# Sums of weight quadrants by accumulating transfers from GpSimd instead of VectorE additions, in one decoder layer on one Trainium2 core

## The chip, the cores and the metric

The kernel runs on one core of one Trainium2 chip. The metric is the device time of one execution in microseconds, the median of three runs. A core has five engines with instruction queues of their own, each in order: TensorE (PE in the profile, with its weight loads as PEld), VectorE (DVE), ScalarE (ACT), GpSimd (POOL) and SyncE (SP, whose queue issues transfers as SPq). They share an on-chip memory, and transfers to and from the large memory are carried by sixteen DMA engines. An engine's instruction waits on semaphores that other engines and transfers raise.

## The reference

One decoder layer on 512 tokens of width 2048, in float32. Cut to what matters here:

```python
mod = silu(c) @ w_ada + b_ada                      # shift, scale, gate
h = rms_norm(x, norm_w) * (1 + scale) + shift
proj = h @ w_in                                    # 2048 -> 21056 channels
a_out = swa_attention(...) * silu(ag)              # 32 query heads, window 128
y_a = a_out @ w_o_swa
o = gated_delta_rule(dq, dk, dv, g, beta)          # 16 key heads, 32 value heads, chunks of 64
y_b = (rms_norm(o, dn_norm_w) * silu(dz)) @ w_o_dn # 4096 -> 2048
y = sigmoid(mg_a) * y_a + sigmoid(mg_b) * y_b
out = x + gate * (y @ w_out)                       # 2048 -> 2048
```

## The kernel before

The 512 tokens lie on the free axis and the channels on the partitions. A channel tile (`channel_tile`) is 128 channels of `h @ w_in`: 16 blocks of the contraction, and for each three matmuls of 128x512 (`mm3`, L255 to L257), since a float32 product is made of a high and a low part (high x high, high x low, low x high). The weights come as 1 MB tiles `raw` (L213, two buffers), and ScalarE and VectorE split each half into `whi` and `wlo` (L61, L62; three buffers) ahead of use. TensorE's order is written out by the program; the rest of the work hangs beside it: `channel_tile` calls `pump` after every sixth matmul, eight times a tile, and `pump` steps generators. `go` starts one that asks for a delay in calls at each yield. `paced` starts one with a budget: each call adds the budget to a purse, and a step is taken when the purse holds what the last yield asked for. A recording layer then orders the instructions of each engine's queue and puts in the semaphores.

The stages in order: start-up (`h`, first tiles), keys of the delta rule with a triangular solve, attention, delta heads, the product with `w_o_dn`, the products with `w_o_swa` and `w_out`. The change is in the delta heads (`delta_heads`): 16 groups `g`, each with five channel tiles (one of queries, two of values, two of gates) and, beside them, its work: loads of the decay rows `E`, masks of them on GpSimd (L742), exponentials on ScalarE (L748), products with `pqk` on VectorE (L886), loads of `qe` and products `qe` on GpSimd (L880), small loads `tt`, `ta`, `lab`, `ts`, loads `k` and `kT`, and a scan over four chunks (`pp`, `pv`, `pod`); `ptq` is the transpose of the group's queries, once a group. `o_d` is where a group's result is stored.

The products with `w_o_dn` (in two halves) and `w_out` are made of seven smaller products each (`PRODUCTS`), on 2x2 blocks of the matrices, where four of the seven need a sum of weight blocks: with quadrants 00, 10, 11, 01 the sums are f0 = 00 + 10, f1 = 10 + 11, f2 = 00 + 10 + 11, f3 = all four. `weight_sums` makes them during the delta heads, from group 3 on, and stores them in `g_d` and `f_d`, from where the later stages load them as they load weights. A unit of it is one half of the columns (1024) of one block: four quadrant tiles `q` of 128x1024 are loaded by SP (L1193), VectorE adds (L1198, in place), and SP stores each sum (L1200). There are 24 units, with a budget of 2.0 a call. `behind` ties an instruction's place in its queue to the last matmul recorded, without a semaphore.

Of the kernel before, what the change touches and what calls it, by code (L numbers as in the profile page):

```python
# [7 lines left out]
F32 = mybir.dt.float32  # L8
# [3 lines left out]
ALU = mybir.AluOpType  # L12
# [4 lines left out]
P = 128  # L17
# [28 lines left out]
class Layer:  # L46
# [603 lines left out]
    def delta_heads(self):  # L650
        tc, nc = self.tc, self.nc
        with ExitStack() as sb:
            self.pmm = sb.enter_context(tc.tile_pool(name="pmmh", bufs=2, space=PSUM, reuse_waits="tile"))
            self.ptp = sb.enter_context(tc.tile_pool(name="ptph", bufs=3, space=PSUM, reuse_waits="tile"))
            self.psc = sb.enter_context(tc.tile_pool(name="psch", bufs=3, space=PSUM, reuse_waits="tile"))
            self.gwk = sb.enter_context(tc.tile_pool(name="gwkh", bufs=1, reuse_waits="tile"))
            wk = sb.enter_context(tc.tile_pool(name="dnB", bufs=2, reuse_waits="tile"))
            self.tt = []
            for n in range(4):
                t = wk.tile([P, NTB, P], F32, tag=f"tt{n}", name=f"tt{n}", bufs=1)  # L660
                nc.gpsimd.memset(t[HD:P, :, 0:HD], 0.0)
                self.tt.append(t)
            while not self.solved:
                self.step_slow(self.solves)
            ws = sb.enter_context(tc.tile_pool(name="wsum", bufs=1, reuse_waits="tile"))
            sums = None
            for g in range(KH):
                if g == 3:
                    sums = self.paced(self.weight_sums(ws), 2.0)
                if g == 8:  # L670
                    self.drain_slow(self.solves)
                self.heads(wk, g)
            for j in range(9, 12):
                self.merge_gate("ma", j, self.ma_d)
            self.drain_live()
            self.drain_slow(sums)

    def solve_all(self):
        for b in range(2):
# [498 lines left out]
            self.split(self.hh[:, kt, :], self.hl[:, kt, :], raw)  # L1178
            yield 1.2

    def weight_sums(self, wk):

        nc, a = self.nc, self.a
        sets = [(a["w_od"][0], self.g_d[0]), (a["w_od"][1], self.g_d[1]), (a["w_out"], self.f_d)]
        for w, dst in sets:
            for n in range(2):
                for i in range(2):
                    for h in range(2):
                        cols = slice(h * 1024, (h + 1) * 1024)
                        q = []  # L1190
                        for c, r in ((0, 0), (1, 0), (1, 1), (0, 1)):
                            t = wk.tile([P, 1024], F32, tag=f"q{c}{r}", name=f"q{c}{r}", bufs=1)
                            self.behind(nc.sync.dma_start(out=t, in_=w[2 * c + n, 2 * r + i][:, cols]))  # L1193
                            q.append(t)
                            yield 1.0
                        yield 8.0
                        for f, (x, y) in enumerate(((0, 1), (1, 2), (0, 2), (2, 3))):
                            self.behind(nc.vector.tensor_tensor(out=q[f], in0=q[x], in1=q[y], op=ALU.add))  # L1198
                            yield 6.0
                            self.behind(nc.sync.dma_start(out=dst[n, f, i][:, cols], in_=q[f]))  # L1200
                        yield 7.0

    def rope_tables(self, wk, keep):
        nc, a = self.nc, self.a
# [507 lines left out]
```

## Time and profile before

| what | value |
|---|---|
| runs | 2870.41, 2878.47, 2881.50 us; median 2878.47 |
| the profiled execution | 2872.04 us, its span 2870.2 us |
| TensorE busy, share of the span | 2820.4 us, 98% |
| VectorE busy | 1969.6 us, 69% |
| ScalarE busy | 1188.4 us, 41% |
| GpSimd busy | 141.6 us, 5% |
| DMA | 604.28 MB, mean 211 GB/s |
| additions of the sums (L1198) | 96, 124.5 us, from 1265.6 to 2118.5 us |
| loads and stores of the sums (L1193, L1200) | 96 and 96, 0.5 MB each |

The span runs from the first to the last instruction of the profiled execution; the execution's own time lies 1.8 us above it. The matmuls' ends are modelled, so that a busy TensorE is not one at its pace; the pace shows in the distance from one matmul to the next. The DMA share is the mean busy share of the sixteen DMA engines.

### The profile page before, as it was taken

How to read it: one execution, taken by the hardware profiler on the slowest of the kernel's cores; microseconds unless marked ns; L12 is line 12 of the kernel's file. 1: busy time of each engine (PE TensorE's matmuls, PEld its weight loads, DVE VectorE, ACT ScalarE, POOL GpSimd, SP SyncE). 2: the span in 40 equal slices, each digit the busy share in tenths (PEclk: the TensorE clock that was granted, in tenths of full speed). 3: DMA queues.
4: the chain of work that ended last, by engine and by line, in shares of the span. 5: the costliest groups of instructions: out<-in, count | busy, mean ns of one | idle time of the engine just before them, and what ended most of it. 6: DMA issues, size and time to landing. Idle time of an engine off the chain costs nothing.

```text
span 2870.2 us, 38671 instructions
## 1 busy us (share of the span) xinstructions
PE 2820.4 (98%) x14396; PEld 2314.6 (81%) x14396; DVE 1969.6 (69%) x3174; ACT 1188.4 (41%) x2382; POOL 141.6 (5%) x124
## 2 busy tenths in 40 slices
PE   7899999999999999999999999999999999999999
PEld 6588888877877778888788888888888888878887
DVE  7776776868768766778676666665656776664576
ACT  4356443234444343433433333333334454433443
POOL 0001000100001000001000000000000000000000
PEclk9999999999999999999999999999999999999999
DMA  9777864322252343456777676666646887885784
GB/s 398 289 250 235 257 231 143 112 89 90 80 159 81 110 151 99 134 170 233 236 261 246 229 241 232 235 236 228 231 171 226 288 314 258 295 281 175 245 317 165
DMA packets 227727, 604.28 MB, mean 211 GB/s; under 512 B 76081, under 2 KB 102193, under 8 KB 187089
## 3 DMA queue, kind: packets, MB, share of 16 engines
q1 hardware_dynamic: 227538, 601.81, 62.0%
q8 instruction: 113, 1.85, 0.3%
q14 instruction: 76, 0.62, 0.1%
HBM read 481.32 MB, written 118.17 MB: 209 GB/s over the span
## 4 chain that ended last, share of the span: by engine, by line
PE 87%; DVE 5%; DMA 3%; ACT 2%; issue 1%; SPq 0%; POOL 0%; DVEq 0%; POOLq 0%; ACTq 0%
PE mm L255 20%; PE mm L257 20%; PE mm L256 20%; PE m L256 5%; PE m L255 5%; PE m L257 5%; DVE wa L437 1%; DVE wlo L62 1%; PE pv L933 1%; DMA E<-g_rows 1%; PE S L1389 1%; PE pod L952 1%; PE O L1440 1%; PE pP L296 1%; ACT sm L1413 1%
## 5 line engine op out<-in xcount | busy, mean ns | idle before, releaser
L255 PE MATMUL mm<-hh,whi 128*128 128x512 f32 x2784 | 1130.1, 406 | 2.8 <-ACT mth L285 2.8
L257 PE MATMUL mm<-hh,wlo 128*128 128x512 f32 x2784 | 1089.5, 391 | 0.0
L256 PE MATMUL mm<-hl,whi 128*128 128x512 f32 x2784 | 1086.9, 390 | 0.0
L62 DVE TENSOR_TENSOR wlo<-raw,whi 128x1024 fp32r<-128x1024 f32 (+1 forms) x532 | 655.2, 1232 | 425.0 <-ACT whi L61 409.6
L61 ACT CAST whi<-raw 128x1024 fp32r<-128x1024 f32 (+1 forms) x532 | 555.4, 1045 | 848.6 <-PE mm L256 612.2
L255 PEld LDWEIGHTS mm<-hh,whi 128*128 128x128 f32 x2784 | 523.5, 188 | 113.6 <-issue 9.2
L257 PEld LDWEIGHTS mm<-hh,wlo 128*128 128x128 f32 x2784 | 522.6, 188 | 113.6 <-issue 0.5
L256 PEld LDWEIGHTS mm<-hl,whi 128*128 128x128 f32 x2784 | 524.0, 188 | 100.4 <-issue 1.4
L1198 DVE TENSOR_TENSOR q<-q,q 128x1024 f32<-128x1024 f32 x96 | 124.5, 1297 | 0.2 <-DMA q<-in_w_od 0.2
L748 ACT ACTIVATE E<-E,neg_g 128x128 f32<-128x128 f32 x256 | 82.1, 393 | 88.7 <-POOL E L742 88.6
L777 DVE TENSOR_TENSOR atmp<-A 128x62 f32<-128x62 f32 (+30 forms) x124 | 109.7, 884 | 0.5
L785 DVE TENSOR_TENSOR A<-A,atmp 128x62 f32<-128x62 f32 (+30 forms) x124 | 109.1, 880 | 0.4
L880 POOL TENSOR_TENSOR qe<-qe,yq 128x512 f32<-128x512 f32 x32 | 50.9, 1608 | 940.2 <-DMA qe<-eg_rows 624.3
L953 ACT COPY osb<-pod 128x256 f32<-128x256 f32 x64 | 23.8, 372 | 149.9 <-PE pod L952 149.9
L742 POOL TENSOR_SCALAR_AFFINE_SELECT E<-E 128x512 f32<-128x512 f32 x64 | 60.0, 950 | 430.7 <-DMA E<-g_rows 307.2
L935 ACT COPY vn<-pv 128x256 f32<-128x256 f32 x64 | 23.8, 372 | 120.8 <-PE pv L933 120.8
L1413 ACT ACTIVATE sm<-sm,mx,rs 128x256 f32<-128x256 f32 (+1 forms) x128 | 71.7, 562 | 3.5 <-DVE mx L1408 3.5
L604 DVE SCALAR_TENSOR_TENSOR yv<-mm,convh,yv 128x511 f32<-128x511 f32 (+2 forms) x96 | 71.4, 743 | 1.2
L940 DVE TENSOR_SCALAR vs<-vn,kd 128x128 f32<-128x128 f32 x96 | 23.1, 283 | 60.6 <-ACT vn L935 60.6
L437 DVE SCALAR_TENSOR_TENSOR wa<-wa,silu_cb 128x2048 f32<-128x2048 f32 x24 | 54.8, 2283 | 0.0
L963 DVE SCALAR_TENSOR_TENSOR S<-S,egl,pod 128x128 f32<-128x128 f32 x64 | 19.3, 343 | 50.8 <-ACT junk L956 50.8
L609 ACT ACTIVATE th<-yv 128x512 f32<-128x512 f32 x32 | 20.1, 628 | 72.7 <-DVE yv L604 72.7
(427 smaller groups left out, 3684.4 us busy)
## 6 DMA issues: line engine op xcount, KB each, us to landing
raw<-in_w_ch SPq DMA_DIRECT2D x158, 1024.0 KB
wa<-in_w_ada_ss SPq DMA_DIRECT2D x32, 1024.0 KB
q<-in_w_od SPq DMA_DIRECT2D x64, 512.0 KB
g_d<-q SPq DMA_DIRECT2D x64, 512.0 KB
raw<-g_d SPq DMA_DIRECT2D x32, 1024.0 KB
raw<-in_w_od SPq DMA_DIRECT2D x24, 1024.0 KB
gw<-in_w_ada_gate SPq DMA_DIRECT2D x16, 1024.0 KB
E<-g_rows SPq DMA_DIRECT2D x64, 256.0 KB
```

Source lines behind the costliest of these rows:

```text
L61: self.nc.scalar.copy(out=hi, in_=src)
L62: self.nc.vector.tensor_tensor(out=lo, in0=src, in1=hi.bitcast(F32), op=ALU.subtract)
L255: nc.tensor.matmul(ps, lhsT=wh, rhs=xh, start=first, stop=False)
L256: nc.tensor.matmul(ps, lhsT=wh, rhs=xl, start=False, stop=False)
L257: self.last_mm = nc.tensor.matmul(ps, lhsT=wl, rhs=xh, start=False, stop=last)
L437: nc.vector.scalar_tensor_tensor(out=wa, in0=wa, scalar=0.5, in1=scb, op0=ALU.mult, op1=ALU.mult, accum_out=t[:, j : j + 1])
L604: nc.vector.scalar_tensor_tensor(out=y[:, s:], in0=ps[:, : T - s], scalar=w[:, j : j + 1], in1=y[:, s:], op0=ALU.mult, op1=ALU.add)
L748: self.nc.scalar.activation(E[:, c, :], E[:, c, :], AF.Exp, bias=self.neg_g[:, c, h : h + 1])
L777: eng.tensor_tensor(out=t, in0=A[:, m : m + 1, m + 1 :].to_broadcast([P, m, n]), in1=A[:, :m, m : m + 1].to_broadcast([P, m, n]), op=ALU.mult,
L785: self.behind(eng.tensor_tensor(out=A[:, :m, m + 1 :], in0=A[:, :m, m + 1 :], in1=t, op=ALU.add))
L1198: self.behind(nc.vector.tensor_tensor(out=q[f], in0=q[x], in1=q[y], op=ALU.add))
L1413: nc.scalar.activation(t, t, AF.Exp, scale=r[:, h : h + 1], bias=mx[:, h : h + 1], accum_out=den[:, h : h + 1])
```

## The change

`weight_sums` is split in two generators, one for each half of the columns, and each walks the twelve blocks by itself, with a budget of 1.5. In each, two tiles are used for each block: tile 0 is loaded with quadrant 00, and quadrants 10, 11 and 01 are added to it one after another by transfers that accumulate into the tile as they land (`accum_op`), issued from GpSimd's queue; after each, the tile is stored (f0, f2, f3). Tile 1 is loaded with 10 and accumulates 11 (f1). VectorE has no part in it. A block's half has now two plain loads, four accumulating transfers and four stores, where a unit had four loads, four additions on VectorE and four stores. The tiles take the same space.

```diff
@@ delta_heads
-            sums = None
+            sums = []
             for g in range(KH):
                 if g == 3:
-                    sums = self.paced(self.weight_sums(ws), 2.0)
+                    sums = [self.paced(self.weight_sums(ws, p), 1.5) for p in range(2)]
...
-            self.drain_slow(sums)
+            for e in sums:
+                self.drain_slow(e)
@@ weight_sums
-    def weight_sums(self, wk):
+    def weight_sums(self, wk, part):
...
-                    for h in range(2):
-                        cols = slice(h * 1024, (h + 1) * 1024)
-                        q = []
-                        for c, r in ((0, 0), (1, 0), (1, 1), (0, 1)):
-                            t = wk.tile([P, 1024], F32, tag=f"q{c}{r}", name=f"q{c}{r}", bufs=1)
-                            self.behind(nc.sync.dma_start(out=t, in_=w[2 * c + n, 2 * r + i][:, cols]))
-                            q.append(t)
-                            yield 1.0
-                        yield 8.0
-                        for f, (x, y) in enumerate(((0, 1), (1, 2), (0, 2), (2, 3))):
-                            self.behind(nc.vector.tensor_tensor(out=q[f], in0=q[x], in1=q[y], op=ALU.add))
-                            yield 6.0
-                            self.behind(nc.sync.dma_start(out=dst[n, f, i][:, cols], in_=q[f]))
-                        yield 7.0
+                    cols = slice(part * 1024, (part + 1) * 1024)
+                    quad = lambda c, r: w[2 * c + n, 2 * r + i][:, cols]
+                    q = [wk.tile([P, 1024], F32, tag=f"q{part}{k}", name=f"q{part}{k}", bufs=1) for k in range(2)]
+                    load = lambda k, c, r: self.behind(nc.sync.dma_start(out=q[k], in_=quad(c, r)))
+                    add = lambda k, c, r: self.behind(nc.gpsimd.dma_start(out=q[k], in_=quad(c, r), accum_op=ALU.add))
+                    store = lambda k, f: self.behind(nc.sync.dma_start(out=dst[n, f, i][:, cols], in_=q[k]))
+                    load(0, 0, 0)
+                    load(1, 1, 0)
+                    yield 9.0
+                    add(0, 1, 0)
+                    yield 3.0
+                    add(1, 1, 1)
+                    yield 6.0
+                    store(0, 0)
+                    yield 3.0
+                    store(1, 1)
+                    yield 6.0
+                    add(0, 1, 1)
+                    yield 9.0
+                    store(0, 2)
+                    yield 9.0
+                    add(0, 0, 1)
+                    yield 9.0
+                    store(0, 3)
+                    yield 9.0
```

TensorE's instructions stand in the same order in both kernels. On GpSimd's queue the delta heads are, before, an alternation of masks of `E` and products `qe`, two of each a group (here from the first groups):

```order
L661 MEMSET tt_9191 64x4x64
L742 AFFINE_SELECT E<-E 128x512 x4
L880 TENSOR_TENSOR qe<-qe,yq 128x512 x4
L742 AFFINE_SELECT E<-E 128x512 x2
L880 TENSOR_TENSOR qe<-qe,yq 128x512 x2
```

Now the 96 accumulating transfers (the DMA rows; `q_15120` is tile 0 of one half of the columns, `q_15124` that of the other, `q_15121` and `q_15125` are their tiles 1) stand among them, mostly behind a pair of masks and ahead of the next products. At two places late in the stage, around the change from `w_o_dn` to `w_out`, it reads:

```order
L1193 DMA q_15120<-in_w_od 128x1024
L1193 DMA q_15124<-in_w_od 128x1024
L881 TENSOR_TENSOR qe<-qe,yq 128x512
L1193 DMA q_15121<-in_w_od 128x1024
L1193 DMA q_15125<-in_w_od 128x1024
L881 TENSOR_TENSOR qe<-qe,yq 128x512
L743 AFFINE_SELECT E<-E 128x512 x2
```
```order
L881 TENSOR_TENSOR qe<-qe,yq 128x512 x2
L1193 DMA q_15735<-in_w_out 128x1024
L1193 DMA q_15739<-in_w_out 128x1024
L743 AFFINE_SELECT E<-E 128x512
L1193 DMA q_15736<-in_w_out 128x1024
L1193 DMA q_15740<-in_w_out 128x1024
L743 AFFINE_SELECT E<-E 128x512
```

What moved: masks and products that followed each other directly now have transfers between them that wait for a load of theirs.

SP's queue in one late group before, with loads and stores of the sums spread among the others (`q_14366` and its like are the four quadrant tiles of a unit):

```order
L213 DMA raw<-in_w_ch 128x2048 x2
L1200 DMA g_d<-q_14366 128x1024
L1200 DMA g_d<-q_14368 128x1024
L876 DMA k<-k_d 128x512
L840 DMA kT<-kT_d 128x512
L1200 DMA g_d<-q_14376 128x1024
L865 DMA tt_9185<-ts_d 64x4x64 x2
L213 DMA raw<-in_w_ch 128x2048
L1200 DMA g_d<-q_14378 128x1024
L859 DMA qe<-eg_rows 128x512 x2
L737 DMA E<-g_rows 128x512
L1193 DMA q_14668<-in_w_od 128x1024
```

and at the same kind of place now, from the load of `raw` ahead of `qe` on:

```order
L213 DMA raw<-in_w_ch 128x2048
L860 DMA qe<-eg_rows 128x512 x2
L738 DMA E<-g_rows 128x512 x2
L866 DMA tt_9185<-ts_d 64x4x64 x2
L866 DMA tt_9187<-ts_d 64x4x64
L213 DMA raw<-in_w_ch 128x2048
L994 DMA o_d<-zh 128x512 x2
L1194 DMA g_d<-q_14513 128x1024
L1194 DMA g_d<-q_14517 128x1024
L866 DMA tt_9187<-ts_d 64x4x64
L1194 DMA g_d<-q_14514 128x1024
L1194 DMA g_d<-q_14518 128x1024
```

The stores now come in pairs, each waiting for an accumulating transfer, and the loads that follow them in the queue (the next are `ta`, `lab` and `raw`) stand behind these waits.

## The prediction

> **What bounds the kernel now.** I read the page first: the busy shares of the engines and the chain that ended last.
>
> ```profile
> span 2870.2 us, 38671 instructions
> ...
> PE 2820.4 (98%) x14396; PEld 2314.6 (81%) x14396; DVE 1969.6 (69%) x3174; ACT 1188.4 (41%) x2382; POOL 141.6 (5%) x124
> ...
> PE 87%; DVE 5%; DMA 3%; ACT 2%; issue 1%; SPq 0%; POOL 0%; DVEq 0%; POOLq 0%; ACTq 0%
> ...
> L1198 DVE TENSOR_TENSOR q<-q,q 128x1024 f32<-128x1024 f32 x96 | 124.5, 1297 | 0.2 <-DMA q<-in_w_od 0.2
> ```
>
> TensorE holds 87% of the chain; VectorE, whose 96 additions (L1198) leave, holds 5%. A busy PE need not be a PE at its pace, so I went on to the pace of the stage in which the sums are made. The second view is the chain in order of time, cut to 1251 to 2120 us; its columns are start, duration, and what. `ptq` is issued once in each group of heads.
>
> ```profile
> 1281.87 0.44 PE ptq L296 x4
> ...
> 1349.11 0.44 PE ptq L296 x4
> ...
> 1380.17 1.14 DVE q L1198
> ...
> 1420.00 6.62 DMA E<-g_rows
> ...
> 1442.84 13.24 DMA q<-in_w_od
> 1456.17 1.24 DVE q L1198
> ...
> 1487.54 0.44 PE ptq L296 x4
> ...
> 1623.09 9.68 DMA E<-g_rows
> ...
> 1690.04 0.44 PE ptq L296 x4
> ...
> 1757.28 0.44 PE ptq L296 x4
> ...
> 1824.52 0.44 PE ptq L296 x4
> ...
> 1891.76 0.44 PE ptq L296 x4
> ...
> 1959.81 7.94 DMA E<-g_rows
> ...
> 1968.38 2.21 POOL E L742 x2
> ...
> 2094.47 0.44 PE ptq L296 x4
> ```
>
> From 1690.04 on, three groups in a row take 67.24 us to the hundredth: that is TensorE's own pace for a group. From 1281.87 to 2094.47 lie 812.60 us and twelve groups; twelve times 67.24 is 806.88. So this stage loses **5.7 us** in all, and 138.43 - 2 x 67.24 = 3.95 of them between 1349.11 and 1487.54. TensorE's instructions stand in the same order in both kernels, so 5.7 us is also what the change can give back here. (About 0.5%, 14 us, is what a measurement of this kernel can tell from no change.)
>
> The third view gives the busy time by stretches; the numbers that I use are the share of the sixteen DMA engines and the GB/s at the end of a row.
>
> ```profile
> 1251.00:1445.00 194.00, 191.09 (x1014) 158.78 (x1013) 148.29 (x245) 81.38 (x184) 16.35 (x12) 1.00 0.71 235
> 1445.00:1690.00 245.00, 244.23 (x1279) 203.85 (x1279) 154.22 (x248) 93.06 (x219) 15.82 (x12) 1.00 0.71 238
> 1690.00:1958.00 268.00, 268.00 (x1418) 223.49 (x1417) 169.01 (x281) 104.70 (x248) 19.89 (x16) 1.00 0.70 238
> 1958.00:2120.00 162.00, 161.27 (x871) 134.21 (x870) 107.74 (x179) 61.31 (x146) 14.39 (x10) 1.00 0.68 225
> ...
> 1796.00:1802.00 6.00, 6.00 (x30) 5.02 (x29) 2.83 (x6) 2.42 (x4) 0.00 (x0) 1.00 0.99 388
> ```
>
> The DMA engines are what has least to spare beside TensorE: 194 x 0.71 + 245 x 0.71 + 268 x 0.70 + 162 x 0.68 = 609 us of the 869. The granted clock is 1.00 throughout, so it takes no part.
>
> **The change, part by part.** *VectorE.* 96 additions of 1.297 us leave, 124.5 us. They lie beside TensorE's matmuls; bounds of what comes back are 0 and 5.7 us. Two of them stand in the chain where the 3.95 us were lost, but next to them a load of 13.24 us. I take **-2 us**.
>
> *The amount of transfer.* Before, a unit loads four half-megabyte tiles and stores four: 96 loads and 96 stores. Now 48 loads, 96 accumulating transfers and 96 stores. In the last row above, six microseconds of weight loads and such loads, the engines move 388 GB/s at a share of 0.99, so a plain 0.524 MB takes 0.524 / 388 = 1.35 us of all sixteen. No row shows an accumulating transfer. Least: it costs what a plain load costs, factor 1. Nearest: it reads a row as the load does and reads the tile out as the store does, factor 2. Most, if nothing in it overlaps (read, read, write back): factor 3, and more if it is cut into small pieces. The DMA time of the stage is then 609 - 48 x 1.35 + 96 x 1.35 x factor: 674 us (share 0.78) at factor 1, **804 us (0.92)** at 2, 933 us at 3, which is 64 us more than the stage has. The limit is at 2.5. I take 2.
>
> The Trainium skill, page "DMA: Bandwidth & Descriptors", section "Issuing engines are not separate DMA queues", says that transfers run on the same sixteen engines whichever engine starts them. It speaks against the change: the extra reads meet the weight loads. If what GpSimd starts ran apart, the shared engines would fall to 609 - 48 x 1.35 = 544 us, 0.63, and nothing would come late. No row here has a second data queue. The page "Collectives: The Full Stack", section "The bandwidth ceiling: the fold count and why AG ≠ RS ≠ AR", puts an adding transfer at half the rate of a copy, for its two source reads; that is factor 2 and 0.92, where the plain load's row alone would give 0.78.
>
> *The SP queue.* 48 issues go. The stores' wait changes from VectorE's sum to the landing of an accumulating transfer; behind a waiting store stand on SP the loads of `raw`, `ta`, `lab` and the stores of `o_d`. Who waits now is in the view of SP's own waits (total, times, longest), and in that of the tile `raw` over the same stretch:
>
> ```profile
> SPq L213 <- DVE wlo L62: 122.7, 29, 10.7
> SPq L1200 <- DVE q L1198: 107.8, 40, 6.2
> ...
> SPq L1193 <- DMA g_d<-q: 25.6, 8, 4.9
> ```
> ```profile
> its engine sat idle before it (us, times) until:
>   PE mm L256: 179.0, 82
>   ACT whi L61: 117.6, 89
> ```
>
> SP already stands 107.8 us for the sums, up to 6.2 at a time, and no split of `raw` waited for a load: 40 such waits cost TensorE next to nothing. The same cover hides the new wait as long as a transfer lands in the room that its pace leaves. A group is 5 tiles of 8 pacing calls, so a call is 67.24 / 40 = 1.68 us; a unit's yields add up to 63 at 1.5 a call: 42 calls, 70.6 us (before 43 / 2.0 calls, 36 us, with half the columns). Along chain 0 come one load, three accumulations and three stores, one after another. With 8 us for each plain landing (mean of the three `E` landings above) 32 us go, and each accumulation has 12.8 us. The slowest plain load in the chain took 13.24 us. That is tight, but enough at factor 2: two at a time are 5.4 us of engine time. I take **+0**, and if the cover is gone it is the second rival below.
>
> *The GpSimd queue.* 96 DMA issues join 141.6 us of work. An issue costs at least what it costs on SP, at most what a whole pass over a tile costs here:
>
> ```profile
> L1193 SPq DMA_DIRECT2D q<-in_w_od x64: 323/424/2372, 1251.1 to 1801.0; - x64
> ```
> ```profile
> 1696.36 2.56 POOL L880 TENSOR_TENSOR qe<-qe,yq 128x512 f32<-128x512 f32 x2 [59.56 <-DMA qe<-eg_rows]
> 1698.86 1.62 POOL L742 TENSOR_SCALAR_AFFINE_SELECT E<-E 128x512 f32<-128x512 f32 x1
> 1710.67 0.63 POOL L742 TENSOR_SCALAR_AFFINE_SELECT E<-E 128x512 f32<-128x512 f32 x1 [10.19 <-DMA E<-g_rows]
> ```
>
> So 0.42 to 1.3 us each, 41 to 123 us in all, in an engine that sat 59.56 us idle ahead of these two products. The queue is in order, though: an accumulation whose load or store has not landed holds the products `qe` and the masks of `E` behind it, and ScalarE's `exp` of `E` and VectorE's product with `pqk` follow the masks. How late may a mask be? In the group of 1690.04 the second mask ended at 1711.30, 21 us after the group began; in the one that began at 1891.76 + 67.24 = 1959.0 both were done at 1970.59, after 12 us. And yet the `ptq` behind the later mask came 67.24 us after its own. So about 10 us of lateness costs nothing. In most groups the accumulations stand between the masks and the next products, where the queue was idle; in three groups (two of them are shown with the change: the ones around the first `in_w_out` sums) they stand right between products and masks. There a load of 8 us and two to four issues may use up the 10 us: bounds 0 and 5 us a group, I take 2, and 6 us for the three.
>
> *Sum.* -2 + 0 + 6 = **+4 us** on the profiled execution's 2872.0 (span 2870.2 and 1.8 around it), 2876. The median of the runs, 2878.5, lies 6.4 above it; on that footing the forecast is **2882 us**, no change.
>
> **The rivals.** *First, slower by one mechanism: the accumulations are dearer than factor 2.5.* Then the DMA engines, and with them the chains, no longer fit in the stage: stores wait on SP for landings, `raw` comes late, and TensorE waits. At factor 3 the stage grows by 933 - 869 = 64 us to 2943; at 4 by 1063 - 869 = 194 us to 3073. For it: the share is already 0.7, and no row prices such a transfer. Against it: nothing in the rows makes it more than a load and a store. Chance 0.22.
>
> *Second, slower by the order on GpSimd.* Load landings of 13 us like the one above, issues of 1.3 us, and masks that are late beyond 10 us in every group rather than three: 3 us a group over 13 groups is 39 us, 2917. For it: in the last groups all eight accumulations stand between two pairs of masks. Against it: the 59.56 us idle. It decides from 10 us of lateness on. Chance 0.16.
>
> *Third, faster.* VectorE's relief gives back the whole 5.7 us and no new wait costs anything: 2873. That is still no change by the bound; more would have to come from outside this stage, where the change touches nothing, or from scatter among the runs (2870 to 2882 before). Chance of over 0.5% faster: 0.05.
>
> **How the numbers follow.** Same 0.57 (the forecast, with the third rival inside it), slower 0.22 + 0.16 = 0.38, faster 0.05. The likeliest's own range is 2866 to 2896. To hold eight of ten, the range goes up through the second rival and the first at factor 3: 2866 to 2950; left out are factors above 3 and a lucky measurement.
>
> **What would show it.** Groups at 67.24 us between `ptq` and `ptq` with accumulations in flight: the forecast. DMA share of the stage: 0.92 says factor 2, 0.78 factor 1, near 1.0 with groups of 72 us and more the first rival. Masks on GpSimd later than 21 us into the group, with ScalarE waiting for `E`: the second. SP's waits at the stores (L1194) under 110 us: the cover holds; several hundred: it is gone. The forecast is wrong if any split of `raw` waits for its load in many groups.

## The result, and the profile after

The changed kernel takes 2897.22 us (2894.64 to 2898.42) where the kernel before takes 2877.48 us (2870.41 to 2881.50): a ratio of **1.0069**, interval 1.0053 to 1.0084. It is slower by 0.7%, 20 us.

The page of the changed kernel: span, engines, the queue that GpSimd feeds, the accumulating transfers as work of GpSimd's queue, and their time from issue to landing.

```profile
span 2896.6 us, 38698 instructions
...
PE 2830.3 (98%) x14396; PEld 2322.5 (80%) x14396; DVE 1858.0 (64%) x3078; ACT 1189.3 (41%) x2382; POOL 216.4 (7%) x220
...
q0 software_dynamic: 13824, 50.34, 9.4%
...
L1193 POOL DMA_DIRECT2D q<-in_w_od x64 | 56.1, 909 | 446.9 <-DMA q<-in_w_od 235.6
...
q<-in_w_od POOLq DMA_DIRECT2D x64, 512.0 KB, 9.9
```

VectorE did lose its additions (1969.6 to 1858.0 us busy). The span is 26.4 us longer than before (2870.2).

Where the time went is read from the chain of waits of the changed kernel, from the same transposes `ptq` as before (start, duration, what):

```profile
1280.32 0.44 PE ptq L296 x4
...
1571.64 10.40 DMA E<-g_rows
1582.19 0.63 POOL E L743
1583.16 0.97 ACT E L749 x3
1584.12 0.94 ACT whi L61
...
1587.66 0.80 PE ptv L296 x4
...
1711.60 18.84 DMA E<-g_rows
...
1785.09 0.44 PE ptq L296 x4
...
2121.34 0.44 PE ptq L296 x4
```

From the first to the last of these `ptq` lie 841.02 us, twelve groups; before it was 812.60. So 28.4 us were lost between the same matmuls, and outside this stage the kernels differ by some 2 us the other way. From 1280.32 to 1785.09 us lie seven groups and 504.77 us, 34.1 more than seven times TensorE's own 67.24. From 1785.09 to 2121.34 lie five groups and 336.25 us, 0.05 more than five times 67.24. So all of the loss is in the first seven groups, in six of them (the one from 1426.60 us on took 67.24), and the same transfers go on for five more at no cost. The lost pieces read much alike: a load lands late (`E` after 10.4 and 18.8 us, where the three on the chain of before took 6.62, 9.68 and 7.94; in the group with the longest stop it is `qe`, for which GpSimd stood 10.48 us, with the masks right behind its products), the mask on GpSimd follows, ScalarE's exponentials of `E` follow the mask, and then come, as the next rows of ScalarE's queue, the conversion `whi` of a weight half or the work on a value tile, on which TensorE stands (at `pu` by way of VectorE, whose copy `Y` stands behind that work). SP is not late: in these six groups it issued both loads of `E` within 3.3 us of the group's first `ptq`. Six stops of TensorE of 3.09, 4.27, 6.02, 3.72, 1.69 and 5.22 us stand in these groups (the distances between neighbouring matmuls, at `pu` and `ptv`).

Now stretches of the changed kernel; the two numbers ahead of the last are the granted clock and the DMA share.

```profile
1251.00:1800.00 549.00, 526.48 (x2718) 438.44 (x2717) 286.65 (x530) 206.97 (x478) 83.03 (x88) 0.98 0.88 256
1800.00:2150.00 350.00, 350.00 (x1869) 291.48 (x1868) 182.16 (x327) 134.53 (x316) 56.79 (x58) 1.00 0.89 259
...
1301.00:1309.00 8.00, 5.29 (x30) 4.02 (x29) 7.21 (x13) 1.56 (x2) 1.75 (x2) 0.79 0.76 134
1376.00:1384.00 8.00, 6.91 (x31) 5.61 (x32) 6.36 (x12) 1.56 (x2) 1.76 (x2) 0.57 0.77 141
1509.00:1520.00 11.00, 5.73 (x16) 4.55 (x16) 6.76 (x9) 5.30 (x11) 1.74 (x2) 0.69 0.97 266
1587.00:1592.00 5.00, 4.34 (x14) 3.59 (x15) 4.86 (x7) 1.86 (x3) 0.00 (x0) 0.66 1.01 224
1734.00:1742.00 8.00, 5.07 (x26) 4.16 (x27) 6.02 (x10) 2.10 (x4) 1.77 (x2) 0.57 1.04 303
```

Two things stand here. The DMA share is 0.88 in the groups that lose and 0.89 in those that don't, so the mean share doesn't tell them apart. And with each stop of 3 us and more the granted clock falls to half, for 3.41 or 6.83 us: 8 x 0.21 + 8 x 0.43 + 11 x 0.31 + 5 x 0.34 + 8 x 0.43 = 13.7 us of full pace are missing in these five rows. That is the most that the clock can have cost, since a part of it falls within the stops themselves.

### The profile page after: what moved, and what is told of

It reads as the page before. It is cut to its first block, busy times and chain, and to the rows that moved or that the text cites. A ratio compares the mean times of both kernels' runs of the same rounds, so it can differ in the third digit from the quotient of the medians.

```text
span 2896.6 us, 38698 instructions
## 1 busy us (share of the span) xinstructions
PE 2830.3 (98%) x14396; PEld 2322.5 (80%) x14396; DVE 1858.0 (64%) x3078; ACT 1189.3 (41%) x2382; POOL 216.4 (7%) x220
## 3 DMA queue, kind: packets, MB, share of 16 engines
q0 software_dynamic: 13824, 50.34, 9.4%
## 4 chain that ended last, share of the span: by engine, by line
PE 87%; DMA 5%; DVE 5%; ACT 2%; issue 1%; SPq 0%; POOL 0%; DVEq 0%; POOLq 0%; ACTq 0%
PE mm L255 20%; PE mm L257 20%; PE mm L256 20%; PE m L256 5%; PE m L255 5%; PE m L257 5%; DMA E<-g_rows 2%; DVE wlo L62 1%; PE S L1401 1%; DVE wa L437 1%; PE pv L934 1%; PE pod L953 1%; PE O L1452 1%; PE pP L296 1%; PE pp L924 1%
## 5 line engine op out<-in xcount | busy, mean ns | idle before, releaser
L1193 POOL DMA_DIRECT2D q<-in_w_od x64 | 56.1, 909 | 446.9 <-DMA q<-in_w_od 235.6
L743 POOL TENSOR_SCALAR_AFFINE_SELECT E<-E 128x512 f32<-128x512 f32 x64 | 53.0, 839 | 430.3 <-DMA E<-g_rows 377.1
L1257 POOL TENSOR_TENSOR aq<-aq,cos 128x512 f32<-128x512 f32 x16 | 25.1, 1570 | 340.3 <-DMA partner<-aq 310.4
```

The source lines that it names most:

```text
L1193: add = lambda k, c, r: self.behind(nc.gpsimd.dma_start(out=q[k], in_=quad(c, r), accum_op=ALU.add))
```

## The experiments

### The accumulations themselves, or the order on GpSimd

Theory A said that the accumulations keep the DMA engines busy and other loads land late behind them. Theory B said that the order on GpSimd, with accumulations that wait between masks and products, is what makes the masks late. The first kernel leaves the queue as it is and moves an eighth of the columns:

```diff
-   add = ... dma_start(out=q[k], in_=quad(c, r), accum_op=ALU.add)
+   add = ... dma_start(out=q[k][:, :128], in_=quad(c, r)[:, :128], accum_op=ALU.add)
```

> The 96 accumulating transfers stay in GpSimd's queue at the same places and with the same waits, but each moves 128 of its 1024 columns (the sums are left incomplete in the other columns). Theory A (the extra bytes make the loads of E, qe and raw land late, and these hold TensorE): the six stops of 1.7 to 6.0 us in the delta heads go, groups of 67.24 us, DMA share of the stage near 0.7, span 2868 to 2875, time 2870 to 2880. Theory B (the order in GpSimd's queue: accumulations that wait for their loads and stores hold the products and masks): four or more stops of over 3 us stay, span 2888 to 2897.

2872.01 us, ratio 0.9988 (0.9978 to 0.9999). That speaks against B, since each issue took as long as before. The order is not quite the same, though: some of GpSimd's rows stand otherwise in four groups.

```profile
L1193 POOL DMA_DIRECT2D q<-in_w_od x64 | 56.2, 941 | 435.3 <-DMA q<-in_w_od 236.6
```

The second moves the whole columns from GpSimd, but as plain transfers:

```diff
-   add = ... dma_start(out=q[k], in_=quad(c, r), accum_op=ALU.add)
+   add = ... dma_start(out=q[k], in_=quad(c, r))
```

> The 96 transfers from GpSimd overwrite the tile instead of adding to it (so the sums are not sums); their number, queue, order and waits stay. Theory A with a cost of two plain transfers for an accumulation: DMA share of the stage falls from 0.89 to about 0.80, landing from 9.9 us to 7 or 8, stops shrink to half or less, span 2872 to 2885. If an accumulation costs what a plain load costs, share and span stay (0.89, 2893 to 2899). Theory B: span stays at 2893 to 2899 whatever the share.

2872.43 us, ratio 0.9991 (0.9981 to 1.0002). Here the rows of all engines stand in exactly the order of the changed kernel, and the twelve groups take 811.4 us instead of 841.0: B falls.

```profile
q0 software_dynamic: 13824, 50.34, 5.2%
...
L1193 POOL DMA_DIRECT2D q<-in_w_od x64 | 34.6, 541 | 440.0 <-DMA q<-in_w_od 234.1
...
q<-in_w_od POOLq DMA_DIRECT2D x64, 512.0 KB, 7.0
```

For the same 50.34 MB the queue took 5.2% of the engines' span here and 9.4% with accumulation: an accumulating transfer costs 1.8 times a plain one. It lands after 9.9 us instead of 7.0, and its issue holds GpSimd for 0.91 us instead of 0.54. A stands so far, but not as a matter of the amount alone: five groups of the changed kernel bear the same amount without loss.

### The place of the burst in the group

The unit of a chain lasts 42 calls and a group 40, so the unit's dense beginning (two loads, two accumulations, two stores a chain) drifts through the group. Theory C: only where in the group it falls decides. Both kernels here make the unit exactly one group long (budget 1.575) and begin it 20, or 8, calls later:

```diff
-   sums = [self.paced(self.weight_sums(ws, p), 1.5) for p in range(2)]
+   sums = [self.paced(self.weight_sums(ws, p), 1.575) for p in range(2)]
...
+   yield 20.0 * 1.575
    for w, dst in sets:
```
```diff
+   yield 8.0 * 1.575
    for w, dst in sets:
```

> All work stays; the chains' period is made one group (63 / 1.575 = 40 calls) and their start is put 20 calls later, half a group. Theory C (the stops come from the point of the group at which a unit's burst falls: the changed kernel drifts by 2 calls a group and lost nothing from its eighth unit on, 16 calls behind the start): every unit falls where the last four fell, no stop over 3 us, groups of 67.24, span 2868 to 2875, same as the kernel before. Theory A without a role for the point of time: share 0.89 as it was, and half of the groups or more with a stop: span 2890 to 2900.

> As the run with 20 calls, but a start 8 calls later, in the middle of the drift in which the changed kernel lost 34 us over seven groups. Theory C: nearly every one of the twelve groups with a unit loses 3 to 8 us: span 2905 to 2950. Theory A alone: the same as with 20 calls. Theory B: the order in GpSimd's queue here has all accumulations between masks and the next products in each group, so few stops, span 2870 to 2885.

20 calls later: 2881.45 us, ratio 1.0025 (1.0015 to 1.0035). Eight calls later: 2950.13 us, ratio 1.0260 (1.0235 to 1.0286). The work is the same, and 69 us lie between them: the place counts, as C says. With 20 calls, all groups of the profile but two keep 67.24 us; these two put the span at 2877.4 us, above the 2868 to 2875 expected. With eight, every group from 1283 to 2172 us takes 72.1 us or more, and the chain shows much the same rows in each, here one:

```profile
1587.74 11.71 DMA E<-g_rows
...
1600.62 0.97 ACT E L749 x3
1601.60 0.94 ACT whi L61
...
1605.13 0.87 PE ptv L296 x4
```

The place also changes the recorded order of ScalarE: with eight calls four of a group's exponentials stand ahead of its second `whi`, with 20 calls all eight stand behind it in most groups. So these two kernels don't tell how much the place does by traffic and how much by order.

One of the two other groups of the first kernel took 76.27 us. There the end of the second triangular solve copies its result on ScalarE in four pieces through a single buffer, and each copy waits for the store of the piece ahead of it:

```profile
1395.36 5.94 DMA ta_d<-atmp
1401.38 1.91 ACT atmp L791
1403.29 0.28 ACT vn L936
```

Again a late transfer, an instruction of ScalarE that waits for it, and behind it the copy `vn` that TensorE needs.

Is the size of the transfers part of it? The kernel of eight calls with plain transfers:

```diff
+   yield 8.0 * 1.575
...
-   add = ... dma_start(out=q[k], in_=quad(c, r), accum_op=ALU.add)
+   add = ... dma_start(out=q[k], in_=quad(c, r))
```

> The same kernel with the burst 8 calls later, E where it was, but the transfers that GpSimd issues are plain ones that overwrite (the sums aren't made: each store writes the last quadrant). DMA time of that queue falls to about 1/1.8. Theory C with the accumulation's size as its cause: half of the lateness goes, few stops above 3 us, 2875 to 2900. If only the place of the transfers in the group counts and not their size: 2930 to 2950 as with accumulation.

2891.47 us, ratio 1.0068 (1.0053 to 1.0083), where accumulations took 2950.13 us: size and place both count, as the first half of the expectation had it. All engines' rows stand in the same order in these two kernels, so what the size does is not a matter of order. One stretch of it, around a stop of 2.54 us at `ptv`:

```profile
1577.00:1585.00 8.00, 7.23 (x39) 5.67 (x40) 6.04 (x10) 2.41 (x4) 0.00 (x0) 0.79 0.95 315
```

The stops are shorter now, 2.77 us at most, but the clock still fell behind this one (the one of 2.77 us left it alone).

### E sooner: an edit that didn't move it

If a late `E` is the cause, an earlier load should help:

```diff
-   yield from self.conv(wk, ps, g, q)
    M = [self.decay_load(wk, 2 * g + e) for e in range(2)]
+   yield from self.conv(wk, ps, g, q)
```

> The changed kernel, its sums and their pace untouched; only the two loads of E of a group are issued ahead of the query's convolution (four calls, some 6.7 us, sooner) instead of behind it. Theory C (E lands late where the burst of the sums is, and the masks, the exponentials on ScalarE and at last TensorE wait for it): the stops of TensorE that the chain of waits leads back to E (before 1377.09, 1587.66 and 1736.93 us, 4.27 + 3.72 + 5.22 = 13.2 us, with half clock for 6.83 + 3.41 + 6.83 us behind them, 8.5 us lost) go or shrink under 2 us; the one behind raw (1514.27 us, 6.02 us) stays. 2897 falls to 2875 to 2882. Theory D (the traffic of that stretch delays whatever comes next in line, so another load takes E's place): stops stay of 3 us or more in most groups, 2890 to 2900.

> The kernel whose burst comes 8 calls later in each group (2950), with the same edit: E is issued ahead of the query's convolution. All work is there. Theory C: E, which took 11.6 us to land from 1513.85 us and was on the chain ahead of each of its stops at ptv, is in time, the stops of 3.5 to 5.4 us in each group go, 2950 falls to 2880 or less. Theory D: another load holds the same chain, 2930 to 2955.

2897.88 us (ratio 1.0088, 1.0074 to 1.0102) and 2951.81 us (1.0277, 1.0261 to 1.0293): nothing gained. But this is no verdict on E, because the edit did not move it. SP's queue in the first of the two kernels:

```profile
1563.18 0.83 SPq L860 DMA_DIRECT2D qe<-eg_rows x2
1564.07 1.45 SPq L738 DMA_DIRECT2D E<-g_rows x2
```

The `ptq` of that group started at 1563.8 us: `E` is still issued right behind `qe`, at the start of the group, as in the changed kernel (at 1571.04, the group having begun at 1569.53). Something other than the place in the code holds it there, and that led to the next view, of everything on the tile `E` from 1040 to 1165 us, in the changed kernel (count, duration, first and last start):

```profile
L749 ACT ACTIVATE E<-E,neg_g x24: 386/388/406, 1054.4 to 1156.2; 128x128 f32<-128x128 f32 x24
...
L738 SPq DMA_DIRECT2D E<-g_rows x6: 382/416/737, 1048.9 to 1146.4; - x6
...
L887 DVE TENSOR_TENSOR E<-pqk,E x4: 680/682/684, 1094.1 to 1163.4; 128x512 f32<-128x512 f32 x4
```

Two loads, eight exponentials and two products (L887) belong to a group. By 1165 us there are loads and exponentials of three groups, but products of two. **E is loaded, masked and exponentiated one whole group ahead of its use.** The kernel before shows the same counts. There are four buffers, two a group, so a pair can be loaded as soon as the group before last has finished with it, and the recording layer puts the mask and the exponentials as early as that allows. So ScalarE stands waiting, in order, for a result that nobody needs for 67 us, and the `whi` and `yv` behind it, which TensorE needs at once, come late.

### The exponentials held in their own group

Theory E says that this wait is the loss; theory D, that the traffic in that stretch is too much whatever waits for it. The edit ties the exponentials of a group to their own place in the program, as the sums and the `qe` products are:

```diff
-   def decay_exp(self, E, h):
+   def decay_exp(self, E, h, held=False):
        for c in range(NTB):
-           self.nc.scalar.activation(E[:, c, :], E[:, c, :], AF.Exp, bias=...)
+           (self.behind if held else id)(self.nc.scalar.activation(E[:, c, :], E[:, c, :], AF.Exp, bias=...))
...
-   self.decay_exp(M[e], 2 * g + e)
+   self.decay_exp(M[e], 2 * g + e, True)
```

The orders of TensorE and of GpSimd stay as they are in the change. In ScalarE's list a group's eight exponentials now stand in one place, between its second and third `whi`, where the place varied from group to group in the changed kernel; and each `E` is one group older.

> The changed kernel with one thing held: ScalarE's eight exponentials of E of a group stay behind the weight products of that group. In the changed kernel, as in the kernel before, E's loads, masks and exponentials run a whole group ahead of their use, since each of them may start as soon as its buffer is free (from the second group on, ScalarE's exponentials of 1154 us belong to the multiplication at 1230 us). ScalarE's list reads the same, but each row's E was loaded one group (67 us) earlier. All work, the sums, their pace and the order on GpSimd are as in the change. Theory E (ScalarE stands at exponentials that nobody needs for a group, and the conversions of the weights behind them come late): with nothing to wait for, the stops of 3 us and more between 1280 and 1785 us go, 2897 falls to 2868 to 2878. Theory D (the traffic itself is too much for that stretch; raw, qe or kT are late on their own account): stops remain, 2888 to 2900.

> The same hold in the kernel whose burst comes 8 calls later (2950), where every group from 1300 us on stops for 3.5 to 5.4 us and the chain leads from each stop through whi and the exponentials to a mask and a load of E. Theory E: 2950 falls to 2870 to 2885. Theory D: 2930 to 2950.

In the changed kernel: **2867.80 us, ratio 0.9966 (0.9956 to 0.9977)**, 29 us less than without the hold. With the burst at the bad place: 2878.41 us, ratio 1.0008 (0.9998 to 1.0018), 72 us less. Theory E holds and D falls. The changed kernel with the hold, by stretches, by the first and the last start of `ptq`, by its `E` up to 1165 us, and ScalarE's exponentials on the page:

```profile
1251.00:1800.00 549.00, 548.39 (x2900) 457.42 (x2899) 305.95 (x554) 221.60 (x510) 93.69 (x96) 1.00 0.93 273
```
```profile
L296 PE MATMUL ptq<-ident,yq x52: 272/273/273, 1278.8 to 2086.9; 128*128 128x128 f32 x52
```
```profile
L749 ACT ACTIVATE E<-E,neg_g x16: 386/388/392, 1086.7 to 1157.7; 128x128 f32<-128x128 f32 x16
```
```profile
L749 ACT ACTIVATE E<-E,neg_g 128x128 f32<-128x128 f32 x256 | 80.3, 392 | 19.8 <-POOL E L743 17.0
```

The DMA share in the stretch that lost 34 us is now higher, 0.93 for 0.88, and the clock stays at 1.00. By 1165 us there are sixteen exponentials, two groups' worth. ScalarE waits 17.0 us for masks in the whole program; the same row of the changed kernel, and of the one with the burst eight calls later, had

```profile
L749 ACT ACTIVATE E<-E,neg_g 128x128 f32<-128x128 f32 x256 | 81.9, 393 | 96.4 <-POOL E L743 96.2
```
```profile
L749 ACT ACTIVATE E<-E,neg_g 128x128 f32<-128x128 f32 x256 | 82.1, 392 | 149.8 <-POOL E L743 149.7
```

The total does not tell what a wait costs: the kernel before has nearly as much of it as the changed kernel.

```profile
L748 ACT ACTIVATE E<-E,neg_g 128x128 f32<-128x128 f32 x256 | 82.1, 393 | 88.7 <-POOL E L742 88.6
```

What counts is how much of it falls in one group. In the changed kernel ScalarE stood 6.2 to 10.5 us for masks in each of the six groups that lost time, and 4.8 us or less in the six that did not; with the burst eight calls later it stood 9.0 to 11.0 us in all twelve; with the hold, 0.0 in all twelve. The masks come no earlier for it: the second one of a group ends 9.4 to 20.8 us after the group began with the hold, and 9.4 to 20.6 us without. Accumulations land after 10.0 us. It is only that nobody urgent waits for them any more.

Could the new place of the exponentials, and not the older `E`, have done it? Two groups of the changed kernel, those of 1280.16 and 1642.02 us, have them in that very place. ScalarE stood 6.73 and 6.15 us for the masks there, and the groups lost 4.3 and 1.4 us. So the place alone is not enough.

### Which part of the gain is whose

Two candidates to beat both kernels, both with the burst 20 calls later and the solve's four copies in two buffers of their own (in `self.spare`, the pool of the sums); the second has the hold, the first the edit that was to move `E` (which did not move it here either):

```diff
-   tmp = wk.tile([P, 1024], F32, tag="atmp", name="atmp", bufs=1)
+   tmp = (self.spare if b else wk).tile([P, 1024], F32, tag="acp" if b else "atmp", name="atmp", bufs=2 if b else 1)
```

> A candidate to beat both. The sums as in the kernel with the burst 20 calls later (2881.5: all groups at 67.24 us but two beside the end of the solve, 76.27 and 69.17), the four copies of the second solve in two buffers of their own so that ScalarE doesn't wait for their stores, and E ahead of the convolution. All work is there. If the two groups lost their 9 and 2 us to these waits, 2868 to 2873, against 2877 of the kernel before (at most 5.7 us can come from VectorE's relief); if the stores of the solve merely stand for any traffic there, 2878 to 2882.

> A candidate to beat both: the burst 20 calls later, two buffers of their own for the second solve's four copies, and the exponentials held. All work is there. Theory E and the bound on VectorE's relief (5.7 us at most): 2867 to 2872, a ratio of 0.997 to 0.999 to the kernel before. If only the place of the burst counts, the hold adds nothing to it: 2873, as without the hold (2873.07).

Without the hold 2873.07 us, ratio 1.0001 (0.9992 to 1.0010), against 1.0025 with one buffer: the group of 76.27 us is back at 67.24. The one behind it is not cured (69.17 before, 69.65 now), so the waits for the stores explain only the larger of the two losses. With the hold 2869.54 us, ratio 0.9980 (0.9971 to 0.9990). The latter is no better than the hold with the change's own pace (0.9966). The place is not indifferent for all that: at eight calls the hold leaves 1.0008, with groups of 72.87 and 69.13 us beside the solve.

Last, the same hold in the kernel before, with its sums on VectorE:

```diff
-   self.decay_exp(M[e], 2 * g + e)
+   self.decay_exp(M[e], 2 * g + e, True)
```

> The kernel before, its sums on VectorE, with the exponentials of E held in their own group. It tells whether the 0.3% by which the changed kernel with the hold beats the kernel before comes from the sums that left VectorE or from the hold. If from the sums (at most 5.7 us of stage could come from there): this kernel is at 0.999 to 1.001 of the kernel before. If the hold alone does it: 0.996 to 0.998.

2871.07 us, ratio 0.9987 (0.9978 to 0.9996), between the two expectations. The row of `ptq` for the kernel before, and for this one (its two times are the first and the last start, from the first matmul of thirteen groups to the last):

```profile
L296 PE MATMUL ptq<-ident,yq x52: 272/273/273, 1281.7 to 2094.6; 128*128 128x128 f32 x52
```
```profile
L296 PE MATMUL ptq<-ident,yq x52: 272/273/273, 1278.8 to 2089.3; 128*128 128x128 f32 x52
```

By this row the kernel before needs 812.9 us, with the hold 810.5, and with the hold and the sums moved 808.1 (1278.8 to 2086.9, above). So of 4.8 us that come back in this stage, half would come from the hold and half from the sums. This rests on one profiled execution of each kernel. The ratios agree in direction (0.9987 and 0.9966), but their intervals almost touch, and the whole spans of the profiled executions stand the other way round (2863.8 us with the sums on VectorE, 2865.9 with the sums moved). That the moved sums are worth 0.2% is not shown.

## Why the prediction was right or wrong

**The sum came out on the wrong side.** 2882 us, no change, was forecast; 2897 and slower by 0.7% was measured, more than the 0.5% that the prediction took as its bound of no change. The time lies within the stated range of 2866 to 2950, but only by luck: it is just past the 2896 at which the likeliest case ended, and the range went further for the sake of two rivals, neither of which is what happened. The terms one by one:

**GpSimd's queue, +6: the step that failed.** Two of its parts were wrong. The first is where the lateness comes from. It was read from the order on GpSimd, for three groups with accumulations between masks and products. These three, which began at 1426.60, 1784.92 and 1852.16 us, took 67.24 us each and lost nothing. With the same order and plain transfers the loss goes, so it is the landing of `E` and `qe`, beside the accumulations on the DMA engines, that is late, in whichever group the burst falls on it. The second is "about 10 us of lateness costs nothing", read from the group that began at 1690.04 us in the kernel before. Its ScalarE, from that group on (the bracket is the idle time ahead of an instruction and who ended it):

```profile
1700.52 1.28 ACT L748 ACTIVATE E<-E,neg_g 128x128 f32<-128x128 f32 x4 [1.81 <-POOL E L742]
1703.48 1.04 ACT L61 CAST whi<-raw 128x1024 fp32r<-128x1024 f32 x1 [1.68 <-PE mm L256]
...
1711.34 0.99 ACT L748 ACTIVATE E<-E,neg_g 128x128 f32<-128x128 f32 x3 [5.72 <-POOL E L742]
```

The late mask held up only exponentials that stood behind `whi` and `yv`. The other group of that reading, which began at 1959.0 us and whose masks were done after 12 us, has its exponentials ahead of a `whi`, and it took 68.23 us: the group with the early mask lost a microsecond, the one with the late mask nothing.

```profile
1969.05 1.28 ACT L748 ACTIVATE E<-E,neg_g 128x128 f32<-128x128 f32 x4 [6.14 <-POOL E L742]
...
1971.81 1.03 ACT L61 CAST whi<-raw 128x1024 fp32r<-128x1024 f32 x1
```

In the group of 1493.84 us of the changed kernel the eight exponentials stand ahead of them:

```profile
1508.29 2.44 ACT L749 ACTIVATE E<-E,neg_g 128x128 f32<-128x128 f32 x8 [10.37 <-POOL E L743]
1510.63 1.03 ACT L61 CAST whi<-raw 128x1024 fp32r<-128x1024 f32 x1
...
1866.72 0.68 ACT L601 ACTIVATE yv<-mm,convh 128x512 f32<-128x512 f32 x1
1867.30 0.39 ACT L749 ACTIVATE E<-E,neg_g 128x128 f32<-128x128 f32 x1
```

Ten microseconds of wait went straight on to `whi`, and TensorE stood 6.02 us. The last two rows are from a group without loss, the one that began at 1852.16: the order is the harmless one again, as it was in the group from which the rule was drawn. The order alone does no harm either: in the group of 1919.40 us seven exponentials stand ahead of a `whi`, ScalarE stands 4.77 us for their mask, and the group takes 67.29 us. The room of 10 us was a property of ScalarE's order in one group, not of the mask; it has to be read as the time that ScalarE stands ahead of an urgent row, and the limit for that lay between 4.8 and 6.2 us in the changed kernel. In place of 2 us in three groups stand 34.1 us in six others, of which at most 13.7 us are the clock.

**The clock.** "It takes no part" was read from the kernel before, where the longest stop of the stage (at 1404.8 us, 2.88 us) left it alone:

```profile
1400.00:1408.00 8.00, 5.51 (x27) 4.27 (x26) 2.42 (x6) 4.61 (x5) 0.00 (x0) 1.00 0.65 155
```

The stops of 3.09 us and more each brought a stretch of lower clock; that of 1.69 us did not. The limit is no sharp one: in the kernel with plain transfers at eight calls a stop of 2.54 us already brought one (0.79, above), where 2.88 us here did not. The Trainium skill, page "TensorE: Matmul & The Clock Gate", section "Why this matters for your kernels", asks for no gaps beyond about 3 us between bursts of matmuls; the five long stops agree, the one of 2.54 us says that somewhat less can be enough.

**VectorE's relief, -2.** Not contradicted: with ScalarE's wait out of the way two profiled executions differ by 810.5 - 808.1 = 2.4 us in this stage, which is no more than a hint, as said above. In the change itself nothing of it could be seen.

**The amount of transfer, factor 2.** Right. 9.4% of 2896.6 us over 96 accumulations are 2.84 us of all engines for each, against 1.55 us for the plain transfers of the same queue (5.2% of 2866.4 us) and the 1.35 us that the prediction took for a plain one, and the DMA share was 0.88 to 0.89 where 0.92 was forecast. The first rival (dearer than 2.5) falls. But the reading that went with it, a share near 1.0 as the mark of loss, was of no use: groups lost at 0.88 and, with the hold, hardly any time was lost at 0.93.

**SP's queue, +0.** Right. Two rows for the stores in the changed kernel, from 1251 to 2150 us:

```profile
SPq L1194 <- DMA q<-in_w_out: 49.1, 10, 12.9
SPq L1194 <- DMA q<-in_w_od: 44.0, 17, 7.5
```

93.1 us, under the 110 named as the bound. A split waited for `raw` twice in the heads, 10.2 and 8.1 us, not in many groups. (The prediction calls the loss of this cover the second rival; the one that describes it is the first.)

**The rivals.** The second had the right rows (masks late, ScalarE waiting for them) and the wrong cause and size: not the order on GpSimd, and six groups of 1.4 to 8.5 us instead of thirteen of 3. Its sign, masks later than 21 us into the group, never came: in the groups that lost, the second mask ended after 13.9 to 20.6 us. What no rival had was that the late work was not due: the chain of waits names what ended last, never by when it was needed. The view of the tile `E`, which has three groups' exponentials beside two groups' products by 1165 us, would have shown it in the kernel before.

## What to carry to other kernels

Where the chain runs from a late transfer through an in-order engine to the bound engine, ask first when the result of the waiting instruction is used: if that is far off, the wait can be moved behind the urgent work. Here that cost nothing and was worth more than moving the transfers: 29 us against 16 in the changed kernel, and 72 against 69 where the burst stood eight calls later. Compare the counts of a tile's loads, its preparation and its use up to one point in time; they show how far ahead the recorded order runs. Slack is to be read from the order of the engine that waits, in several groups, and a stop of TensorE of some 2.5 us or more is to be priced with the lower clock that may come with it.

## What the hardware showed beside that

An accumulating transfer of 0.5 MB cost 1.8 times the DMA time of a plain one (9.4% against 5.2%), landed 2.9 us later in the same places (9.9 against 7.0 us; 8.4 us where the burst stood eight calls later), and held GpSimd 0.91 us an issue instead of 0.54, even when it moved an eighth of the bytes (0.94). The same work spread differently within a 67 us group cost 0.25% or 2.6%, at shares of the DMA engines that were no guide to it: 0.91 and 0.86 between 1251 and 1800 us.
